# Three experts of a float32 mixture on 64 slots, chosen on the chip, and weight pieces of 1024 columns

## The chip, the core and the metric

The kernel runs on one core of a Trainium2 chip. A time is in microseconds (us) of the device for one execution. The core's engines are TensorE (PE; its weight loads are shown as PEld), VectorE (DVE), ScalarE (ACT), GpSimd (POOL) and SyncE (SP), whose queue issues the weight transfers.

## The reference, cut to what matters

Two decoder layers over 256 tokens of 1024 features; the second layer's channel mixer is a mixture of eight experts, of which each token takes two. In float32:

```
logits = x @ router_w                          # [256, 8]
top_val, top_idx = top_k(logits, 2)
gates = softmax(top_val)
for each token t and each of its two experts e:
    out[t] += gate * (silu(x[t] @ w_gate[e]) * (x[t] @ w_up[e])) @ w_down[e]
x = layer_norm(ALPHA * x + out, ln2_g, ln2_b)
```

`w_gate` and `w_up` are [8, 1024, 3584], `w_down` is [8, 3584, 1024]: 352 MB of float32 for eight experts, each byte read once.

## The kernel before, in words

All weights are split on the chip into a high part, rounded to float32r by ACT (line 173), and the low rest, by DVE (line 176). Tokens are split likewise. A product is the sum of three: high by high, high weights by low tokens, low weights by high tokens (`xstat`, with `mm` at line 97).

Weights come in pieces of 1 MiB (`load`, line 158, on SP's queue) into slots `raw` of rings: 7 slots of `ring`, 7 of `ring2`, and one taken once. `halves` splits a piece into two pairs `wh`, `wl` of 128 x 1024, each with four buffers (`WB`).

Ahead of the experts, `enter_moe` makes the layer norm and the logits, `route` the expert ranks: `place` [token, expert] is 1 plus the token's rank in the expert, or 0. `experts` then goes over experts 0 to 7 in turn. Two experts at a time get their tokens by a product with one-hot slots `D` (`dispatch`), 128 slots each, into `xg`. Of the 3584 inner features a chunk is 512: four pieces of four 128-row blocks by 512 columns for gate (`ps_mm`) and up (`ps_gd`), then silu on ACT (line 1017), the product with up on DVE (1018), four transposes on PE (1024), the split of the transposed `hT` on ACT and DVE (1026, 1027). The down products (`ps_b`, two pieces of two 128-row blocks by 1024 columns) run one chunk late, between these steps. After an expert's last chunk `combine` brings its output back to the tokens by the transposed slots `DT` and adds it, times the gate, to `x_tok` (line 990). The order on each engine follows the program, except where the scheduler moves an instruction that is not pinned.

If some expert has more than 128 tokens, a second pass over the next 128 slots runs behind a branch (lines 1125, 1126).

Of the kernel before, what the change touches and what calls it, by code (L numbers as in the profile page):

```python
# [8 lines left out]
F32 = mybir.dt.float32  # L9
F32R = mybir.dt.float32r  # L10
# [6 lines left out]
P = 128  # L17
# [14 lines left out]
# the constant table: identity, 32 rotary frequencies, further [P, P] matrices, then [P, 32] tiles  # L32
# [31 lines left out]
def trunk(ctx, tc, x, positions, w_in, conv_w, a_log, dt_bias, gdn_norm_w, lam_q1, lam_k1, lam_q2, lam_k2,  # L64
# [35 lines left out]
    def wstat(banks, wh, wl, xT, k0, nk, cols, outs):  # L100
        """Feature-major products, weights stationary: outs = (bank, offset, opens the bank) per 128 columns."""
# [27 lines left out]
    def xlast(outs, xT, subs, b, K, k0=0, n0=0):  # L129
        """The last products of block b, one column part after the other; subs: (k, high, low), all of 128 rows."""  # L130
# [8 lines left out]
    extra = []  # ring2, while it is open  # L139
    turn = [0]  # L140
    once = []  # slots to be taken once, after all the others
    fence_high = [None]  # an ACT instruction that further high parts are issued behind
    fence = [None]  # a DVE instruction that further low parts are issued behind

    def load(src, nk, cols, parts=1, cut=1):
        """One piece of weights, [P, nk, cols] in DRAM, comes in; cut: its second half in so many parts of columns."""
        if once and turn[0] == RING + RING2:
            pool = once.pop()
        else:
            pool = extra[0] if extra and SLOTS[turn[0] % len(SLOTS)] == "x" else ring  # L150
            turn[0] += 1
# [11 lines left out]
    def halves(ld, cut=1, count=2):  # L163
        """The halves of a piece, or a small one as a whole: (first k, high part, low part)."""
# [20 lines left out]
    pre_ctx = ExitStack()  # what the layers ahead of the experts need  # L185
# [37 lines left out]
    def xt_block(xT, src, b, on_pe=True, tags=("mm", "gd")):  # L223
        """One block of 128 tokens of src [P, D] goes to feature-major xT."""
# [25 lines left out]
    def layer_norm(xt, halves, par, dst=None):  # L250
        """LN(ALPHA * xt + halves) into dst (or xt[P, D]), halves: two [P, 512] parts; without halves LN(xt)."""
# [18 lines left out]
    def mixer(l, xT, mx, zab=None):  # L270
# [10 lines left out]
        # --- z gate and the a, b columns, token-major: silu(z) * norm weight  # L281
# [19 lines left out]
        # --- gates: beta, log decay, its running sum  # L301
# [13 lines left out]
        V.scalar_tensor_tensor(e1, lg, -1.0, e1, op0=ALU.add, op1=ALU.subtract)  # rounding of 1 + e, negated  # L315
# [8 lines left out]
        gs = gt[:, 4]  # running sum  # L324
# [6 lines left out]
        # --- decays within a chunk of 128, transposed: [j, i] = exp(G_i - G_j), j <= i  # L331
# [24 lines left out]
        # --- from here on in steps, issued in the order that ORDER says  # L356
        # the activation tables: batches of silus, and of exponentials and logarithms, in turn
# [12 lines left out]
        # --- gated-DeltaNet projections, feature-major, then conv + silu  # L370
# [46 lines left out]
        def with_k(y, o):  # L417
            """(y k^T . decay)^T but for the norm of y."""
# [19 lines left out]
        def with_queries():  # L438
# [3 lines left out]
            G.tensor_tensor(egb, gq[:, :, P:], egb, op=ALU.mult)  # q exp(G) of block 1  # L442
# [57 lines left out]
            # blocks of 64  # L500
# [25 lines left out]
            # blocks of 128  # L526
# [13 lines left out]
        # --- attention projections, token-major  # L540
# [44 lines left out]
        # --- differential attention: scores and softmax  # L585
# [3 lines left out]
        def lambdas():  # L589
# [9 lines left out]
            V.tensor_scalar(lam[:, 5:6], lam[:, 4:5], lam_init, None, op0=ALU.subtract)  # -lambda  # L599
# [322 lines left out]
    def experts(xs, gate, place, mp, ring2, rest, first):  # L922
# [72 lines left out]
        for e in range(NE):  # L995
            j = e % 2
            if j == 0:
                xgs = nxt
# [252 lines left out]
```

## Time and profile before

| | us |
|---|---|
| median of 3 runs | 1547.65 |
| lowest and highest | 1545.3, 1548.48 |
| the profiled execution's span, first to last instruction | 1546.8 |

The profiled execution is known by its span, which lies between the lowest and the highest run; the median is 0.9 us above it. In the rows below, a time is counted from the span's start, "x24" is a count of instructions, and "<-" behind an idle time names what ended it. PE's products are pipelined, so that the duration of a single one (394 ns) is longer than the distance from one to the next.

### The profile page before, as it was taken

The page shows a single profiled execution, that of the slowest core. Times are in us where ns is not written, and L with a number is a line of the kernel's source. Part 1 is how long each engine was busy: PE and PEld are TensorE (multiplying, and loading weights), DVE is VectorE, ACT ScalarE, POOL GpSimd, SP SyncE. Part 2 cuts the span into 40 slices and gives each one's busy share as a digit, 9 for nine tenths or more (in the row PEclk, how much of TensorE's full clock was granted, in tenths as well). Part 3 has the DMA queues.
Part 4 walks back from the last instruction along what each step waited for, and adds up shares of the span by engine and source line. Part 5 has one row for each costly group of instructions (what it writes and reads, how often), then busy time and mean ns, then how long its engine had stood idle before and what let it go on. Part 6 is the DMA issues. An engine that isn't in the chain of part 4 may idle for free.

```text
span 1546.8 us, 23384 instructions
## 1 busy us (share of the span) xinstructions
PE 1507.5 (97%) x8952; PEld 1263.1 (82%) x8952; DVE 1249.1 (81%) x1528; ACT 1054.3 (68%) x1456; POOL 23.6 (2%) x36
## 2 busy tenths in 40 slices
PE   7999999999999999999999999999999999999997
PEld 7978899998978888878878878887887887887885
DVE  4797655556796888897898889889989889888987
ACT  3648544456757587777777777777777777777774
POOL 1000000000100000000000000000000000000000
PEclk9999999999999899999999999999999999999998
DMA  9534465546433799999999999999999999999960
GB/s 306 202 98 130 161 200 187 182 126 215 164 111 137 272 340 350 370 335 338 368 334 356 370 345 360 331 373 345 349 370 349 326 362 333 363 373 332 376 248 30
DMA packets 184695, 433.81 MB, mean 280 GB/s; under 512 B 7400, under 2 KB 9576, under 8 KB 184576
## 3 DMA queue, kind: packets, MB, share of 16 engines
q1 hardware_dynamic: 183392, 428.54, 77.5%
q0 software_dynamic: 1184, 3.71, 0.9%
q8 instruction: 72, 1.18, 0.3%
q14 instruction: 47, 0.39, 0.1%
HBM read 431.17 MB, written 1.05 MB: 279 GB/s over the span
## 4 chain that ended last, share of the span: by engine, by line
PE 93%; DVE 3%; ACT 2%; issue 1%; DMA 1%; SPq 0%; DVEq 0%; ACTq 0%
PE ps_b L97 27%; PE ps_mm L97 27%; PE ps_gd L97 27%; PE ps_a L97 9%; PE ps_a L1024 2%; DVE wl L176 1%; DMA x_in<-in_x_dram 1%; ACT wh L173 1%; DVE x_in L990 0%; PE ps_mm L562 0%; ACT junk L411 0%; PE ps_gd L404 0%; PE ps_mm L666 0%; DVE o L1084 0%; ACT junk L651 0%
## 5 line engine op out<-in xcount | busy, mean ns | idle before, releaser
L176 DVE TENSOR_TENSOR wl<-raw,wh 128x1024 fp32r<-128x1024 f32 (+1 forms) x811 | 948.2, 1219 | 131.9 <-ACT wh L173 124.2
L173 ACT ACTIVATE wh<-raw 128x1024 fp32r<-128x1024 f32 (+1 forms) x811 | 830.4, 1058 | 223.4 <-PE ps_gd L97 109.2
L97 PE MATMUL ps_b<-wh,hT 128*128 128x512 f32 x984 | 273.7, 399 | 0.0
L97 PE MATMUL ps_mm<-wh,xg 128*128 128x512 f32 x896 | 248.4, 394 | 0.0
L97 PE MATMUL ps_gd<-wh,xg 128*128 128x512 f32 x896 | 245.2, 394 | 0.0
L97 PEld LDWEIGHTS ps_b<-wh,hT 128*128 128x128 f32 x984 | 180.7, 188 | 38.0
L97 PEld LDWEIGHTS ps_gd<-wh,xg 128*128 128x128 f32 x896 | 168.2, 188 | 39.0
L97 PEld LDWEIGHTS ps_mm<-wh,xg 128*128 128x128 f32 x896 | 167.4, 188 | 37.9
L97 PE MATMUL ps_b<-wl,hT 128*128 128x512 f32 x492 | 155.0, 394 | 0.0
L97 PE MATMUL ps_gd<-wl,xg 128*128 128x512 f32 x448 | 140.6, 395 | 7.1 <-DVE wl L176 7.1
L97 PE MATMUL ps_mm<-wl,xg 128*128 128x512 f32 x448 | 141.3, 394 | 0.2
L1026 ACT ACTIVATE hT<-ps_a 128x512 fp32r<-128x512 f32 x56 | 33.5, 598 | 130.7 <-PE ps_a L1024 130.6
L97 PEld LDWEIGHTS ps_b<-wl,hT 128*128 128x128 f32 x492 | 92.4, 188 | 21.7
L97 PEld LDWEIGHTS ps_gd<-wl,xg 128*128 128x128 f32 x448 | 83.7, 188 | 29.6 <-DVE wl L176 10.2
L97 PEld LDWEIGHTS ps_mm<-wl,xg 128*128 128x128 f32 x448 | 83.7, 188 | 20.7 <-DVE wl L176 1.5
L1018 DVE TENSOR_TENSOR hh<-hh,ps_gd 128x512 f32<-128x512 f32 x56 | 38.5, 687 | 40.4 <-PE ps_gd L97 40.0
L97 PE MATMUL ps_mm<-xT,wh 128*128 128x256 f32 x448 | 71.0, 280 | 0.0
L1027 DVE TENSOR_TENSOR hT<-ps_a,hT 128x512 fp32r<-128x512 f32 x56 | 38.7, 690 | 38.2 <-ACT hT L1026 38.2
L97 PEld LDWEIGHTS ps_mm<-xT,wh 128*128 128x128 f32 x448 | 60.8, 189 | 0.4
L97 PE MATMUL ps_gd<-xT,wh 128*128 128x256 f32 x320 | 50.5, 280 | 0.0
L97 PE MATMUL ps_mm<-xT,wl 128*128 128x256 f32 x224 | 44.7, 280 | 0.0
L97 PEld LDWEIGHTS ps_gd<-xT,wh 128*128 128x128 f32 x320 | 43.1, 189 | 0.0
(370 smaller groups left out, 1519.3 us busy)
## 6 DMA issues: line engine op xcount, KB each, us to landing
raw<-in_moe_w_gate_dram SPq DMA_DIRECT2D x110, 1024.0 KB, 7.5
raw<-in_moe_w_up_dram SPq DMA_DIRECT2D x110, 1024.0 KB, 6.3
raw<-in_moe_w_down_dram SPq DMA_DIRECT2D x108, 1024.0 KB, 7.3
raw<-in_w_in_dram SPq DMA_DIRECT2D x24, 1024.0 KB, 6.0
raw<-in_ffn_w_gate_dram SPq DMA_DIRECT2D x11, 1024.0 KB, 5.1
raw<-in_ffn_w_up_dram SPq DMA_DIRECT2D x11, 1024.0 KB, 5.2
raw<-in_ffn_w_down_dram SPq DMA_DIRECT2D x11, 1024.0 KB, 5.0
raw<-in_w_out_dram SPq DMA_DIRECT2D x8, 1024.0 KB, 5.0
```

The source lines that it names most:

```text
L97: return PE.matmul(o, lhsT, rhs, start=start, stop=stop, skip_group_check=True)
L173: high = S.activation(wh[:, c:c + n], w, AF.Copy)
L176: low = V.tensor_tensor(wl[:, c:c + n], w, wh[:, c:c + n].bitcast(F32), op=ALU.subtract)
L1018: pin(V.tensor_tensor(hh, hh, pgu[1], op=ALU.mult))
L1024: PE.transpose(pt[:, f * P:(f + 1) * P], hh[:, f * P:(f + 1) * P], ident)
L1026: S.activation(hT[:, :, 0], pv, AF.Copy)
L1027: V.tensor_tensor(hT[:, :, 1], pv, hT[:, :, 0].bitcast(F32), op=ALU.subtract)
```

## The change

Narrow experts: the three experts of 1 to 7 that fewest tokens chose are treated with 64 slots, and their stationary tile holds the 64 high and the 64 low token parts side by side, 128 columns. One product with the high and one with the low weights then gives the high tokens' sum in the output's rows 0 to 63 and the low tokens' in rows 64 to 127. For gate and up, ACT copies the lower rows to SBUF and PE adds them to the upper ones by a shift matrix (`lead`); for down, the transposed slots stand twice in `DT`, so that the combination adds both. Low weights by low tokens come into the sum too.

The experts 1 to 7 are sorted by count on DVE (`order_by_count`); SP loads the number of the expert of a rank into a register, by which its weights are addressed. Expert 0 stays first and wide; then come the ranks in the order of `TURN`: 1, 4, 2, 5, 3, 6, 7, the ranks 1 to 3 narrow. `dispatch` is called for groups: expert 0, then [1, 2], [3, 4], [5, 6] and [7] of the turns.

Gate and up pieces are two 128-row blocks by 1024 columns; an expert has three chunks of 1024 columns and one of 512, with four down pieces (two for the last) in each. The rings have 7 and 6 slots, and the slot taken once goes. Behind the experts there are two passes over all of them, each in a branch of its own: for tokens beyond the 64 or 128 slots, and for those 128 further on.

```diff
-RING2 = 7
-SLOTS = "rrrrrxxxrrxxxx"
-RING3 = 1
+RING2 = 6
+SLOTS = "rrrrrxxxrrxxx"
+CHUNKS = (1024, 1024, 1024, 512)
+NARROW = 3
+TURN = (1, 4, 2, 5, 3, 6, 7)
...
+    def gate_pieces():
+
+        n = 2048 // CHUNKS[0]
+        wg = moe_w_gate[0, 0].rearrange("(k p) c -> p k c", p=P)
+        return [piece(wg[:, k:k + n, 0:CHUNKS[0]], n, CHUNKS[0]) for k in (0, n)]
...
+        count = mp.tile([P, NE], F32, name="count")
+        pin(V.tensor_copy(count, pr[:, 16:24]))
...
+        def order_by_count(gate):
+            places, gates, index, beyond = order_by_count.tiles
+            N = NE - 1
+            w = mp.tile([P, 5, N], F32, name="sortw")
+            cn, rk, cs, ix = (w[:, i] for i in range(4))
+            sq = mp.tile([P, 2, N, N], F32, name="sorts")
+            pm = sq[:, 1]
+            def rows(a, n=N):
+                return a.unsqueeze(2).broadcast_to([P, n, n])
+            def cols(a, n=N):
+                return a.unsqueeze(1).broadcast_to([P, n, n])
+            V.tensor_copy(cn, count[:, 1:NE])
+            V.tensor_tensor(sq[:, 0], cols(cn), rows(cn), op=ALU.is_equal)
+            V.tensor_tensor(sq[:, 0], sq[:, 0], tie[:, 0:N, 0:N], op=ALU.mult)
+            V.tensor_tensor(sq[:, 1], cols(cn), rows(cn), op=ALU.is_lt)
+            V.tensor_tensor(sq[:, 0], sq[:, 0], sq[:, 1], op=ALU.add)
+            V.tensor_reduce(rk, sq[:, 0], axis=AX.X, op=ALU.add)
+            V.tensor_scalar(beyond[:, 1:NE], rk, float(NARROW), -64.0, op0=ALU.is_lt, op1=ALU.mult)
+            V.tensor_scalar(beyond[:, 1:NE], beyond[:, 1:NE], float(P), None, op0=ALU.add)
+            V.memset(beyond[:, 0:1], float(P))
+            V.tensor_scalar(rk, rk, 1.0, None, op0=ALU.add)
+            V.tensor_tensor(pm, cols(rk), rows(io1[:, 0:N]), op=ALU.is_equal)
+            V.tensor_tensor(sq[:, 0], pm, cols(io1[:, 0:N]), op=ALU.mult)
+            V.tensor_reduce(ix, sq[:, 0], axis=AX.X, op=ALU.add)
+            V.tensor_copy(index, ix[0:1])
+            for b in range(NB):
+                for to, of in ((places, place), (gates, gate)):
+                    V.tensor_tensor(sq[:, 0], pm, cols(of[:, b, 1:NE]), op=ALU.mult)
+                    V.tensor_reduce(to[:, b, 1:NE], sq[:, 0], axis=AX.X, op=ALU.add)
+            V.tensor_tensor(cn, cn, beyond[:, 1:NE], op=ALU.subtract)
+            V.tensor_reduce(cs[:, 0:1], cn, axis=AX.X, op=ALU.max)
+            V.tensor_scalar(cs[:, 1:2], count[:, 0:1], float(-P), 0.0, op0=ALU.add, op1=ALU.max)
+            V.tensor_tensor(cs[:, 0:1], cs[:, 0:1], cs[:, 1:2], op=ALU.max)
+            most = mp.tile([1, 1], I32, name="most")
+            V.tensor_copy(most, cs[0:1, 0:1])
...
+        C2 = [(sum(CHUNKS[:i]), n) for i, n in enumerate(CHUNKS)]
...
+        def slots(Dt, job, twice=False):
+            _, where, _, narrow = job
+            w = 64 if narrow else P
+            m = 2 if narrow and twice else 1
+            return V.tensor_tensor(Dt.rearrange("p b (m s) -> p b m s", s=w),
+                                   io1[:, 0:w].unsqueeze(1).unsqueeze(1).broadcast_to([P, NB, m, w]),
+                                   where.unsqueeze(3).broadcast_to([P, NB, m, w]), op=ALU.is_equal)
...
+        def in_pieces(w, c0, cols, parts=1, k0=0):
+            nk = 2048 // cols
+            for k in range(k0, KD, nk):
+                for j, wh, wl in piece(w[:, k:k + nk, c0:c0 + cols], nk, cols, parts):
+                    yield k + j, nk // 2, wh, wl
+        def products(outs, xg, narrow, k, nk, wh, wl, cols):
+            if not narrow:
+                xstat(outs, [xg[:, 0:4], xg[:, 4:8]], k, nk, 0, wh, wl, cols, KD)
+                return
+            for j in range(nk):
+                x_ = xg[:, k + j].rearrange("p c s -> p (c s)")
+                for w in (wh, wl):
+                    for i, o in enumerate(outs):
+                        mm(o, x_, w[:, j * cols + i * 512:j * cols + (i + 1) * 512], k + j == 0 and w is wh, False)
...
+        def down(subs, n, c, hT, py):
+            f0 = C2[c][0] // P
+            for f, wh, wl in subs:
+                if jobs[n][3]:
+                    x_ = hT[:, f].rearrange("p c s -> p (c s)")
+                    for w in (wh, wl):
+                        for i, o in enumerate(py):
+                            mm(o, x_, w[:, i * 512:(i + 1) * 512], f0 + f == 0 and w is wh,
+                               f0 + f == FE // P - 1 and w is wl)
...
+        def lead(p, room, i):
+            hi = slice(64, P)
+            o = room[hi, i * 512:(i + 1) * 512]
+            pin(S.activation(o, p[hi, :], AF.Copy))
+            return lambda: mm(p[0:64, :], shift[hi, 0:64], o, False, True)
+        groups = [[0], [1, 2], [3, 4], [5, 6], [7]] if NARROW and rest else [[n] for n in range(NE)]
...
+        for n, job in enumerate(jobs):
+            narrow = job[3]
+            rows = slice(0, 64) if narrow else slice(0, P)
+            xg = xgs.pop(n)
+            wg, wu = (weights(n, i).rearrange("(k p) c -> p k c", p=P) for i in range(2))
+            for c, (c0, cols) in enumerate(C2):
+                nb = cols // 512
+                pg = [bank("mm") for _ in range(nb)]
+                pu = [bank("gd") for _ in range(nb)]
+                parts = 2 if (n, c) == (NE - 1, len(C2) - 1) else 1
+                hh = mp.tile([P, max(CHUNKS)], F32, tag="hh", name=nm("hh"))
+                if narrow:
+                    hT = mp.tile([P, 2, cols], F32R, tag=f"hT{q % 2}", name=nm("hT"))
+                    room = hT[:, 1]
+                    hT = hT[:, 0].rearrange("p (f c s) -> p f c s", c=2, s=64)
+                nk = 2048 // cols
+                begun = [(i * nk + k0, nk // 2, wh, wl) for i, f in enumerate(first or ()) for k0, wh, wl in f]
+                for sub in begun:
+                    products(pg, xg, narrow, *sub, cols)
+                for sub in in_pieces(wg, c0, cols, parts, len(first or ()) * nk):
+                    products(pg, xg, narrow, *sub, cols)
+                first = None
+                moves = []
+                for s, sub in enumerate(in_pieces(wu, c0, cols, parts)):
+                    products(pu, xg, narrow, *sub, cols)
+                    left = KD // (nk // 2) - s
+                    if narrow and left == 3:
+                        moves = [lead(p, room, i) for i, p in enumerate(pg)]
+                    if narrow and left == 2:
+                        for move in moves:
+                            move()
+                downs = down_pieces(pend[0], pend[1], 1) if pend else iter(())
+                subs = next(downs, None)
+                if narrow:
+                    for i, p in enumerate(pg):
+                        pin(S.activation(hh[rows, i * 512:(i + 1) * 512], p[rows, :], AF.Silu))
+                    moves = [lead(p, room, i) for i, p in enumerate(pu)]
+                else:
+                    for i, p in enumerate(pg):
+                        pin(S.activation(hh[:, i * 512:(i + 1) * 512], p, AF.Silu))
+                if subs:
+                    down(subs, *pend)
+                for move in moves if narrow else ():
+                    move()
+                for i, p in enumerate(pu):
+                    h = hh[rows, i * 512:(i + 1) * 512]
+                    pin(V.tensor_tensor(h, h, p[rows, :], op=ALU.mult))
+                if narrow:
+                    subs = next(downs, None)
+                    if subs:
+                        down(subs, *pend)
+                else:
+                    hT = mp.tile([P, cols // P, 2, P], F32R, tag=f"hT{q % 2}", name=nm("hT"))
+                w = 64 if narrow else P
+                nf = 512 // w
+                for f0 in range(0, cols // P, nf):
+                    n_ = min(nf, cols // P - f0)
+                    pt = bank("a")
+                    for f in range(n_):
+                        PE.transpose(pt[:, f * w:(f + 1) * w], hh[rows, (f0 + f) * P:(f0 + f + 1) * P], ident[rows, rows])
+                    pv = pt[:, 0:n_ * w].rearrange("p (f s) -> p f s", s=w)
+                    S.activation(hT[:, f0:f0 + n_, 0], pv, AF.Copy)
+                    V.tensor_tensor(hT[:, f0:f0 + n_, 1], pv, hT[:, f0:f0 + n_, 0].bitcast(F32), op=ALU.subtract)
+                    subs = next(downs, None)
+                    if subs:
+                        down(subs, *pend)
+                for subs in downs:
+                    down(subs, *pend)
+                if pend and pend[1] == len(C2) - 1:
+                    combine(pend[0], q - 1, pend[3], DT)
+                if c == 1:
+                    DT = transposed(n)
+                if c == 2 and n + 1 < NE and n + 1 not in xgs:
+                    group = groups.pop(0)
+                    xgs = dict(zip(group, dispatch([jobs[g] for g in group])))
+                pend = (n, c, hT, py)
+                q += 1
...
+            def expert_of(r):
+                return lambda: nc.values_load(index[0:1, r - 1:r], engines=(mybir.EngineType.SP,), min_val=1, max_val=NE - 1)
+            jobs = every[:1] + [job(expert_of(r), r, places, gates, r <= NARROW) for r in TURN]
+            most = experts(xs, jobs, mp, ring2, then, first)
...
+        for turn_ in range(2 if NARROW else 1):
+            with tc.If(n > turn_ * P):
+                if turn_ or not NARROW:
+                    V.tensor_scalar(place, place, float(-P), None, op0=ALU.add)
+                else:
+                    V.tensor_tensor(place, place, beyond.unsqueeze(1).broadcast_to([P, NB, NE]), op=ALU.subtract)
+                experts(xs, every, mp, ring2, None, None)
```

## Rows read from the trace of the kernel before

**Rows 1.** The page, span and busy time, share, instructions of each engine
```profile
span 1546.8 us, 23384 instructions
...
PE 1507.5 (97%) x8952; PEld 1263.1 (82%) x8952; DVE 1249.1 (81%) x1528; ACT 1054.3 (68%) x1456; POOL 23.6 (2%) x36
```

**Rows 2.** Windows: stretch, its length, busy time by engine, PEclk, DMA share, GB/s
```profile
560.00:1450.00 890.00, 882.69 (x3954) 715.66 (x3953) 786.92 (x751) 671.25 (x761) 0.00 (x0) 1.00 0.97 351
...
603.00:671.00 68.00, 68.00 (x303) 55.25 (x302) 59.75 (x59) 51.06 (x57) 0.00 (x0) 1.00 1.00 367
```

**Rows 3.** The page, the chain that ended last, by engine
```profile
PE 93%; DVE 3%; ACT 2%; issue 1%; DMA 1%; SPq 0%; DVEq 0%; ACTq 0%
```

**Rows 4.** The chain in order of time, 514 to 580: start, us, what
```profile
559.46 0.44 PE ps_a L1024 x4
...
568.25 5.56 PE ps_gd L97 x24
```

**Rows 5.** Timeline of DVE at the first three combinations: start, us, line, what
```profile
668.96 1.41 DVE L990 SCALAR_TENSOR_TENSOR x_in<-ps_a,route,x_in 128x512 f32<-128x512 f32 x2
...
796.08 1.41 DVE L990 SCALAR_TENSOR_TENSOR x_in<-ps_a,route,x_in 128x512 f32<-128x512 f32 x2
...
919.83 1.41 DVE L990 SCALAR_TENSOR_TENSOR x_in<-ps_a,route,x_in 128x512 f32<-128x512 f32 x2
```

**Rows 6.** Groups by form, ACT and DVE, 520 to 1540: busy, mean ns, idle before
```profile
L1026 ACT ACTIVATE hT<-ps_a 128x512 fp32r<-128x512 f32 x56 | 33.5, 598 | 130.7 <-PE ps_a L1024 130.6
L1017 ACT ACTIVATE hh<-ps_mm 128x512 f32<-128x512 f32 x56 | 32.4, 579 | 0.0
...
L176 DVE TENSOR_TENSOR wl<-raw,wh 128x1024 fp32r<-128x1024 f32 x671 | 778.1, 1219 | 28.6 <-ACT wh L173 24.9 <-PE ps_a L97 2.5
L1027 DVE TENSOR_TENSOR hT<-ps_a,hT 128x512 fp32r<-128x512 f32 x56 | 38.7, 690 | 38.2 <-ACT hT L1026 38.2
L1018 DVE TENSOR_TENSOR hh<-hh,ps_gd 128x512 f32<-128x512 f32 x56 | 38.5, 687 | 40.4 <-PE ps_gd L97 40.0
L990 DVE SCALAR_TENSOR_TENSOR x_in<-ps_a,route,x_in 128x512 f32<-128x512 f32 x28 | 19.7, 747 | 4.9 <-PE ps_a L97 4.0
L984 DVE TENSOR_TENSOR ys<-ps_b,ys 128x512 fp32r<-128x512 f32 x14 | 9.6, 683 | 0.0
```

**Rows 7.** Timeline of DVE and ACT, splits issued back to back
```profile
674.02 6.89 DVE L176 TENSOR_TENSOR wl<-raw,wh 128x1024 fp32r<-128x1024 f32 x6
...
1504.98 5.79 ACT L173 ACTIVATE wh<-raw 128x1024 fp32r<-128x1024 f32 x6
```

**Rows 8.** Windows at the filling of the rings, columns as in rows 2
```profile
506.00:512.00 6.00, 6.00 (x28) 4.87 (x27) 4.23 (x7) 0.50 (x2) 0.00 (x0) 1.00 1.04 414
512.00:522.00 10.00, 9.75 (x52) 8.04 (x50) 8.14 (x13) 3.27 (x7) 0.00 (x0) 0.83 1.04 388
```

**Rows 9.** Timeline of SP's queue at the filling of the rings
```profile
503.95 1.35 SPq L158 DMA_DIRECT2D raw<-in_moe_w_down_dram  x2
505.40 1.03 SPq L158 DMA_DIRECT2D raw<-in_moe_w_gate_dram  x2
506.48 6.59 SPq L158 DMA_DIRECT2D raw<-in_moe_w_up_dram  x2
```

**Rows 10.** Timeline of DVE in the routing
```profile
524.85 0.35 DVE L886 TENSOR_TENSOR compare<-compare,tie 128x64 f32<-128x64 f32 x2
```

**Rows 11.** Instructions of the branch's line: ns min/median/max, first and last start
```profile
L1126 SPq EVENT_SEMAPHORE  x8: 17/17/17, 1544.5 to 1545.1; - x8
...
L1126 PEldq COMPARE_BRANCH  x1: 3407/3407/3407, 1531.4 to 1531.4; - x1
...
L1126 SPq COMPARE_BRANCH  x1: 50/50/50, 1541.5 to 1541.5; - x1
```

**Rows 12.** Windows in the second mixer, columns as in rows 2
```profile
450.00:460.00 10.00, 9.43 (x290) 7.21 (x289) 9.29 (x19) 2.26 (x3) 0.00 (x0) 1.00 0.34 109
470.00:480.00 10.00, 10.00 (x56) 8.23 (x56) 6.33 (x19) 7.22 (x22) 0.00 (x0) 0.83 0.22 82
```

More of the change, by code (lines that the diff above doesn't have):

```diff
@@ L145, in load @@
     def load(src, nk, cols, parts=1, cut=1):
[L147 to L151, printed above, removed]
+        pool = extra[0] if extra and SLOTS[turn[0] % len(SLOTS)] == "x" else ring
+        turn[0] += 1
         raw = pool.tile([P, WC], F32, tag="raw", name=nm("raw"))
@@ L853, in enter_moe @@
         logits(0)
-        first = [gate_piece(0, 0, half) for half in range(2)]
+        first = gate_pieces()
         busy(8)
@@ new lines, in route, with experts, xg_tile, dispatch @@
+        if NARROW:
+            sorted_ = mp.tile([P, 2, NB, NE], F32, name="sorted")
+            order_by_count.tiles = (sorted_[:, 0], sorted_[:, 1], mp.tile([1, NE - 1], I32, name="index"),
+                                    mp.tile([P, NE], F32, name="beyond"))
+        return gate, place, rest, order_by_count
+    def experts(xs, jobs, mp, ring2, rest, first):
+        C2 = [(sum(CHUNKS[:i]), n) for i, n in enumerate(CHUNKS)]
+        def xg_tile(narrow):
+            xg_turn[0] += not narrow
+            return mp.tile([P, KD, 2, 64 if narrow else P], F32R, tag="xgn" if narrow else f"xg{xg_turn[0] % 2}", name=nm("xg"),
+                           bufs=1)
+        def slots(Dt, job, twice=False):
[5 more added lines that the diff above has]
+                                   where.unsqueeze(3).broadcast_to([P, NB, m, w]), op=ALU.is_equal)
+        def dispatch(group, early=False):
+            ws = [64 if job[3] else P for job in group]
+            W = sum(ws)
+            Dt = mp.tile([P, NB, W], F32R, tag="hh", name=nm("D"))
+            for j, job in enumerate(group):
+                fence[0] = pin(slots(Dt[:, :, sum(ws[:j]):sum(ws[:j + 1])], job))
+            xgs = [xg_tile(job[3]) for job in group]
@@ L971, in down_piece @@
-        def down_piece(e, c, half, parts=1, cut=1):
-            wd = moe_w_down[0, e].rearrange("(f p) d -> p f d", p=P)
-            return list(piece(wd[:, 4 * c + 2 * half:4 * c + 2 * half + 2, :], 2, D, parts, cut))
-        def down(subs, half, e, c, hT, py):
-            for j, wh, wl in subs:
-                xstat(py, [hT], 2 * half + j, 1, 0, wh, wl, D, FE // P, 4 * c)
-        def combine(e, py, DT):
-            for n in range(2):
-                ys = mp.tile([P, 2, 512], F32R, tag=f"hT{e % 2}", name=nm("ys"))
+            for b in range(NB):
+                PE.transpose(pt[:, b * P:(b + 1) * P], Dt[:, b].bitcast(F32), ident)
@@ new lines, in down_pieces @@
+        def down_pieces(e, c, parts=1, cut=1):
+            wd = weights(e, 2).rearrange("(f p) d -> p f d", p=P)
+            c0, cols = C2[c]
+            for f in range(0, cols // P, 2):
+                last = f == cols // P - 2
+                yield [(f + j, wh, wl) for j, wh, wl in piece(wd[:, c0 // P + f:c0 // P + f + 2, :], 2, D, parts,
+                                                              cut if last else 1)]
+        def down(subs, n, c, hT, py):
[8 more added lines that the diff above has]
+                else:
+                    for w in (wh, wl):
+                        for c_ in range(2 if w is wh else 1):
+                            for i, o in enumerate(py):
+                                mm(o, hT[:, f, c_], w[:, i * 512:(i + 1) * 512], f0 + f == 0 and w is wh and c_ == 0,
+                                   f0 + f == FE // P - 1 and w is wl)
@@ L1042, in experts @@
+                pend = (n, c, hT, py)
+                q += 1
+        _, where, gate, _ = job
+        f0 = C2[c][0] // P
+        subs = [(f0 + f, wh, wl) for subs in down_pieces(n, c, 2, 2) for f, wh, wl in subs]
         extra.clear()
@@ L1100, in experts, with moe @@
         return most
[L1102 to L1113 removed]
+    xg_turn = [0]
+    def moe(xs, pl, first, mp, ring2):
+        gate, place, rest, order_by_count = route(pl, mp)
         def then():
             most = rest()
+            if NARROW:
+                most = order_by_count(gate)
             for b in range(NB):
@@ L1183, in trunk @@
     io1 = cpool.tile([P, P], F32, name="io1")
+    shift = cpool.tile([P, 64], F32R, name="shift") if NARROW else None
     def router_constants():
```

156 lines of the change are left out of this document (49 added, 107 removed).

## Prediction

> **What bounds the kernel now.** I read the page's head first: of a span of 1546.8 us TensorE (PE) is busy for 97%, VectorE (DVE) for 81%, ScalarE (ACT) for less [rows 1]. A PE that is busy on average need not be the bound in the stage that is changed, so I then cut out the eight experts. In the 890 us from 560 to 1450 PE is busy 882.7 us, DVE 786.9, ACT 671.3, the granted clock is 1.00 (2.4 GHz), and the DMA share is 0.97 at 351 GB/s; in an undisturbed stretch of 68 us PE has no gap at all while the transfers run at share 1.00 and 367 GB/s [rows 2]. The reader should see three resources close together: PE full, DMA nearly full, DVE at 88%. The chain that ended last says which one counts: 93% of it is PE [rows 3]. Its pieces give PE's price: 24 products of 512 columns take 5.56 us, 0.232 us each, and the four transposes of a chunk 0.44 us [rows 4]. A chunk of 512 columns has 72 products (24 gate, 24 up, 24 down): 72 x 0.232 + 0.44 = 17.1 us. The pace of whole experts stands in the timeline of DVE, where each expert's first addition to the tokens starts at 668.96, 796.08, 919.83 us [rows 5]: 127.1 us for an expert with a dispatch of the next pair in it, 123.7 without, 250.9 a pair. So what is to be saved is PE work, until DVE or DMA takes over.
>
> **The change part by part: PE.** A narrow expert has its high and low token parts side by side in one stationary tile of 64 + 64 columns, so that a weight row needs two products (with its high and its low part) where it needed three. Per 512 columns that is 48 products instead of 72, plus two products by the shift matrix that add the lower half of gate and up to the upper: 50 x 0.232 + 0.44 = 12.0 us, or 7 x 12.0 + 8 x 0.232 for the combination = 86 us an expert [rows 4]. Three of eight experts fall by some 38 us of PE work. That is not the gain, because the weights are the same bytes and must still be split.
>
> **DVE, the next bound.** Each expert has 84 halves of 1024 columns to split into a low part. One is 1219 ns long [rows 6], but issued back to back six take 6.89 us, 1.148 each [rows 7]. 84 x 1.148 = 96.4. Then 7 products of silu and up at 0.687 (half the partitions, as many columns): 4.8. The low parts of the transposed product are half as wide: three of 512 columns at 0.690 and one of 256, taken as 0.4: 2.5. The combination, 4 x 0.747 + 2 x 0.683: 4.4 [rows 6]. Slots and their transposed copy, two operations of 256 columns: 0.8. Sum 109 us. This is the least that a narrow expert can take. ACT by the same count: 84 high parts at 0.965 (six in 5.79 us [rows 7]), 7 silus at 0.579, 14 new copies out of PSUM ahead of the shift, priced as the silu, 4 + 2 operations at 0.598 [rows 6]: 97 us, below DVE.
>
> **What is late on DVE.** To the 109 us come its waits. The idle columns show 40.4 us before the product with up, 38.2 before the low part of hT and 28.6 before splits over the 56 chunks [rows 6], 1.9 us a chunk. The new wait lies here: ACT's copy of up's lower half waits for PE's last up product, PE's shift for ACT, DVE's product for the shift. Behind ACT's copy stand the high parts of the next down pieces, behind PE's shift the next down products, behind DVE's product the next splits. Laid end to end the path is four products of the last half (0.93), the two copies (1.16), two shifts (0.46), two products (1.37), eight narrow transposes (at most 2 x 0.44 = 0.9 [rows 4]), hT on ACT and DVE (0.6 + 0.69): 6.1 us, against eight down halves, 8 x 1.148 = 9.2 us of splitting, that can be put between its links. A narrow expert now has four chunks (three of 1024 columns, one of 512). From below the waits are nothing (109 us); from above the whole path stands bare in each, 4 x 6.1 = 24 us (133 us). I take 1.25 us a chunk, less than now, because DVE is now the late engine and only its turn-round with PE is left: 5 us, N = 114.
>
> **Wide experts.** Their products, transposes and splits are as many as before, in chunks twice as wide. Nothing is saved. The dispatch goes from pairs of 256 columns to groups of 192, all in wide experts: 3.4 us becomes some 2.6; the last expert's own dispatch gives this back. DVE's clusters (two products, 1.37 us) are covered by the four buffers of split weights, which PE takes 1.39 us each to use (six products). So a pair of wide and narrow takes 123.7 + 2.6 + N and saves 124.5 - N = 10.5 us; three pairs save 31.5.
>
> **Transfers.** A narrow expert's 42 pieces of 1 MiB (44.0 MB) in 114 us ask for 386 GB/s; a pair asks for 88.1 MB in 240 us, 367 GB/s, which the 68 us stretch already holds [rows 2]. The excess inside a narrow expert, 19 GB/s x 114 us = 2.2 MB, is two of the thirteen slots, and the order of turns gives each narrow expert a wide one ahead of it in which to fill them. More is available: when the ring is filled at the start, the window in which down rows (4 KB each) were first in the queue moved 414 GB/s and the next, of gate and up rows (2 KB), 388 [rows 8, 9]. Gate and up in 1024 columns have rows of 4 KB as well. Hence nothing for DMA, its bound being 44.0 / 0.388 = 113.5 us and, by the faster row, 106 us, before any help from the ring. The Trainium skill, "DMA: Bandwidth & Descriptors", section Specifications, puts HBM at about 358 GB/s for a core, against this change: by it a pair could not be under 88.1 / 0.358 = 246 us and a pair would save 4.8, and the time would be 1547.7 - 14.3 + 3.5 = 1537. The trace does not agree over short stretches (414, 388 and 367 GB/s); none of its rows shows such a rate held for hundreds of us.
>
> **Choosing the experts.** The order of counts adds 27 small DVE operations and takes two away, 0.1 to 0.2 us each by operations of 64 columns, where two take 0.35 [rows 10]: 2.5 to 5 us, at the start of expert 0, where DVE already keeps PE's first products waiting. Between nothing (fitted into gaps) and 5 I take 2. The first dispatch, of one expert and not two, halves its copies and columns: 0 to 2.6 us, taken as 1.5 back. SP's load of an expert's number stands ahead of all later weight loads on SP's queue, but the number is ready in the first 20 us of expert 0, and SP comes to it when the 42nd piece is due, some 80 us later: nothing; without that cover, the landing of one transfer, once.
>
> **The end.** There are now two branches around passes that are not run. At the one of before PE's branch took 3.4 us, and SP, last, went on 3.0 us after its own [rows 11]. A second in series costs 0 (if both are fetched together) to 3.4 us, I take 3. The passes are not run: the reference's router, on the inputs as they are drawn, gives 79, 75, 77, 58, 32, 80, 29, 82 tokens, so the three smallest of experts 1 to 7 (29, 32, 58) fit 64 slots and the rest 128.
>
> **Sum.** 1546.8 - 31.5 + 2 - 1.5 + 3 = 1518.8 us in the profiled execution's terms. The median shown, 1547.65, is 0.9 above that span; I carry it over: 1520 us. With N at 109 and the small costs at nothing, 1546.8 - 46.5 - 1.5 + 0.9 = 1500; with N at 118 and the small costs at their upper ends 1546.8 - 19.5 + 8.4 + 0.9 = 1537. That is the forecast's own range.
>
> **Rivals.** (1) Transfers take over. For it: share 0.97 at 351 GB/s over 890 us [rows 2], which scaled to a full share is 362. A pair then takes 88.1 / 0.362 = 243.4 us, saves 7.5, and the time is 1547.7 - 22.5 + 3.5 = 1529. Against it: the share passed 1.00 at 388 and 414 [rows 8]. The figure of the Trainium skill above ("DMA: Bandwidth & Descriptors", Specifications) is this rival's harder form, and its 1537 lies in the range. (2) DVE's waits eat it all: at 3.3 us of idle a chunk N is 122.2, three pairs save 7, the small costs take half and the time is within 3 us of before, 1544. For it: 1.9 a chunk now, and two more links in the path; against it the 9.2 us of splitting to put between. (3) Slower: the path stands bare. From N = 124.4 on (3.9 us a chunk) the kernel is slower by over 3 us; with all 6.1 us N is 133, and the time 1547.7 + 25.5 + 3.5 = 1577. What decides is whether DVE's in-order queue has splits between the product and the low part of hT. (4) The clock. PE would wait some 0.2 us behind each half in a narrow expert. It was granted 1.00 in a stretch of 290 small products with gaps (9.43 of 10 us), and 0.83 in a later one of 56 [rows 12]. At 1.2 GHz a narrow expert's PE work would be 2 x 86 = 172 us, and the time 1547.7 + 3 x 47.5 + 3.5 = 1694.
>
> **How the numbers follow.** Two medians of this kernel are told apart from about 0.2%, 3 us. Chances: forecast 0.58, rival 1 0.19, rival 2 0.08, rival 3 0.12, rival 4 0.03. The first two are faster by over 0.2%, the third is within it, the last two slower: 0.77, 0.08, 0.15. The range from 1500 to 1548 takes in the forecast's range, rival 1 and rival 2, and leaves out rivals 3 and 4 and a little below.
>
> **What would show it.** Right: in the profile after, DVE's first additions to the tokens stand about 126 and 114 us apart in turn; in narrow stretches DVE is busiest (over 0.93), PE has gaps that end with splits, and the DMA rate is above 370 GB/s. The page has some 430 matmuls fewer than 8952 [rows 1]: 3 x 7 x 22, less the 32 of a fifth dispatch. Wrong: narrow stretches of 120 us and more with DVE idle before its product with up or before hT (waits), or with SP free and high parts waiting for landings (transfers), or with a granted clock under 1.00.

## The result, and the profile after

The median fell from 1548.07 us (1545.3 to 1552.62) to 1530.09 us (1529.51 to 1530.5), four runs of each: a ratio of 0.9885, with a 95% interval of 0.9862 to 0.9907. The profiled execution's span is 1528.3 us, 18.5 below that of before; forecast were 28.0. The kernel before is timed anew in every round, on several chips, and its median lies between 1546.6 and 1548.1 us. One execution of e1 below took 1691.2 us at a granted clock of 0.80 and is left out of e1's numbers.

The page's head and its chain by engine:

```profile
span 1528.3 us, 23267 instructions
...
PE 1459.9 (96%) x8522; PEld 1164.7 (76%) x8522; DVE 1248.0 (82%) x1553; ACT 1079.5 (71%) x1494; POOL 23.7 (2%) x36
...
PE 82%; DVE 9%; ACT 4%; issue 2%; DMA 2%; SPq 0%; DVEq 0%; ACTq 0%
```

8952 - 8522 = 430 matmuls fewer, as counted beforehand. Against [rows 1, 3] PE's share of the chain is down from 93 to 82%, and DVE's is up from 3 to 9%: another engine has begun to end waits.

DVE's first additions to the tokens, the pace of whole experts (timeline of DVE):

```profile
684.55 1.40 DVE L1082 SCALAR_TENSOR_TENSOR x_in<-ps_a,route,x_in 128x512 f32<-128x512 f32 x2
798.70 1.40 DVE L1082 SCALAR_TENSOR_TENSOR x_in<-ps_a,sorted,x_in 128x512 f32<-128x512 f32 x2
924.32 1.40 DVE L1082 SCALAR_TENSOR_TENSOR x_in<-ps_a,sorted,x_in 128x512 f32<-128x512 f32 x2
1038.67 1.40 DVE L1082 SCALAR_TENSOR_TENSOR x_in<-ps_a,sorted,x_in 128x512 f32<-128x512 f32 x2
```

The steps are 114.2, 125.6 and 114.4 us where "126 and 114" was written, and a pair is 239.8 where [rows 5] gave 250.9. Such a step runs from the middle of one first chunk to the next, so it mixes two experts. Cut at each expert's first gate product instead, a narrow expert takes 110.1 us and a wide one 128.0 to 131.7. The windows of two narrow experts and of the wide one between them (columns as in [rows 2]):

```profile
657.70:767.90 110.20, 103.80 (x398) 66.03 (x397) 104.69 (x102) 97.23 (x112) 0.00 (x0) 0.98 1.00 384
897.50:1007.60 110.10, 104.42 (x397) 67.11 (x396) 104.61 (x102) 97.40 (x111) 0.00 (x0) 0.97 1.00 385
1007.60:1139.40 131.80, 128.22 (x568) 102.45 (x567) 114.75 (x111) 98.89 (x118) 0.00 (x0) 0.99 0.93 349
```

In the narrow expert DVE is busy 104.6 of 110.1 us (95%), ACT 97.4, and the DMA share is 1.00 at 385 GB/s. DVE and the transfers are nearly full; windows alone can't say which of them sets the 110.1. PE's 104.4 is not work of that size: its column counts each product up to its end, which at full pace is later than the start of the next one, and so short waits do not show in it. They show at the weight loads (PEld) of the same expert, in the timeline and in the waits (us in total, times, longest):

```profile
940.19 0.30 PEld L99 LDWEIGHTS ps_gd<-wl,xg 128*128 128x128 f32 x2 [0.38 <-DVE wl L174]
940.19 0.73 PE L99 MATMUL ps_gd<-wl,xg 128*128 128x512 f32 x2
940.75 0.63 PE L99 MATMUL ps_gd<-wh,xg 128*128 128x512 f32 x2
...
942.94 0.63 PE L99 MATMUL ps_gd<-wl,xg 128*128 128x512 f32 x2
943.41 0.40 PE L99 MATMUL ps_gd<-wh,xg 128*128 128x512 f32 x1
```

```profile
PEld ps_mm L99 <- DVE wl L174: 8.6, 17, 1.7
PEld ps_b L99 <- DVE wl L174: 7.4, 18, 0.8
PEld ps_gd L99 <- DVE wl L174: 7.2, 18, 0.8
```

From 940.19 to the next start two products take 0.56 us, and 0.47 from 942.94, where none waits. In the whole expert the weight loads wait 23.2 us for DVE's low parts. That is the mechanism of the prediction: PE's gaps end with splits.

Where the loss lies, a stretch of PE, ACT and DVE at expert 0's third chunk, in which the next pair's tokens are dispatched (start, us, idle before in brackets), a window over its end, and one over the same row in the next wide expert:

```profile
627.05 1.03 PE L99 MATMUL ps_a<-D,xs 128*128 128x192 f32 x8
...
629.66 0.69 PE L99 MATMUL ps_a<-D,xs 128*128 128x192 f32 x4 [0.70 <-ACT xg L1016]
...
631.05 1.14 PE L99 MATMUL ps_a<-D,xs 128*128 128x192 f32 x8 [0.70 <-ACT xg L1016]
...
633.96 1.96 PE L99 MATMUL ps_mm<-wh,xg 128*128 128x512 f32 x4
...
635.96 1.06 ACT L171 ACTIVATE wh<-raw 128x1024 fp32r<-128x1024 f32 x1 [1.21 <-PE ps_mm L99]
...
637.05 1.23 DVE L174 TENSOR_TENSOR wl<-raw,wh 128x1024 fp32r<-128x1024 f32 x1 [5.24 <-ACT wh L171]
```

```profile
631.00:636.00 5.00, 4.75 (x21) 4.20 (x22) 0.82 (x1) 2.58 (x11) 0.00 (x0) 0.67 1.00 376
...
870.00:875.00 5.00, 3.41 (x25) 2.90 (x24) 2.45 (x2) 4.33 (x15) 0.00 (x0) 1.00 1.01 360
```

The dispatch's 32 products stand in one row on PE and take from 627.05 to 633.96, 6.9 us, because PE waits for ACT to copy each bank into `xg`. Meanwhile no split weights are used up, so ACT's next high part waits for PE and DVE idles 5.24 us; and the granted clock averages 0.67 over the 5 us from 631, so that part of them ran at 1.2 GHz. Behind the gaps four products take 1.96 us instead of 1.09. The clock is the smaller part: the same row in the next wide expert (868.5 to 874.8 us, with the same waits) keeps 1.00 and takes 6.3 us. In the trace of before a dispatch of a pair took turns with gate products (from 720 to 727 us two of them, eight of the dispatch, two, eight, and so on) and cost the 3.4 us between its two kinds of expert [rows 5]:

```profile
720.78 1.11 PE L97 MATMUL ps_a<-D,xs 128*128 128x256 f32 x8
721.73 0.64 PE L97 MATMUL ps_mm<-wh,xg 128*128 128x512 f32 x2
722.21 1.25 PE L97 MATMUL ps_a<-D,xs 128*128 128x256 f32 x8
```

The end, by the second branch's line (ns min/median/max, first and last start):

```profile
L1280 PEldq COMPARE_BRANCH  x2: 3502/4032/4561, 1509.6 to 1513.8; - x2
...
L1280 SPq COMPARE_BRANCH  x2: 45/49/53, 1519.6 to 1523.3; - x2
```

Two branches stand in series. PE's two, 3.5 and 4.6 us, are over by 1518.4, before DVE's last operation ends (1519.20); SP's second comes 3.7 us after its first, behind that end. From DVE's end to the span's end are 9.1 us; before they were 5.6.

### The profile page after: what moved, and what is told of

Its sections match the earlier page's. It is cut to its first block, busy times and chain, and to the rows that moved or that the text cites. A ratio compares the mean times of both kernels' runs of the same rounds, so it can differ in the third digit from the quotient of the medians.

```text
span 1528.3 us, 23267 instructions
## 1 busy us (share of the span) xinstructions
PE 1459.9 (96%) x8522; PEld 1164.7 (76%) x8522; DVE 1248.0 (82%) x1553; ACT 1079.5 (71%) x1494; POOL 23.7 (2%) x36
## 4 chain that ended last, share of the span: by engine, by line
PE 82%; DVE 9%; ACT 4%; issue 2%; DMA 2%; SPq 0%; DVEq 0%; ACTq 0%
PE ps_gd L99 25%; PE ps_mm L99 25%; PE ps_b L99 21%; PE ps_a L99 9%; DVE wl L174 5%; ACT wh L171 2%; DMA raw<-in_moe_w_up_dram 1%; PE ps_a L1168 1%; DMA x_in<-in_x_dram 1%; DVE hT L1171 1%; DVE hh L1155 1%; DVE x_in L1082 1%; ACT xg L1016 0%; PE ps_mm L560 0%; DVE ys L1076 0%
## 5 line engine op out<-in xcount | busy, mean ns | idle before, releaser
L99 PE MATMUL ps_b<-wh,hT 128*128 128x512 f32 x816 | 235.1, 400 | 0.3
L99 PE MATMUL ps_mm<-wh,xg 128*128 128x512 f32 x728 | 216.3, 404 | 2.4 <-ACT wh L171 2.4
L99 PE MATMUL ps_gd<-wh,xg 128*128 128x512 f32 x728 | 207.3, 394 | 0.0
L99 PEld LDWEIGHTS ps_b<-wh,hT 128*128 128x128 f32 x816 | 151.6, 189 | 38.1 <-ACT wh L171 3.1
L99 PE MATMUL ps_b<-wl,hT 128*128 128x512 f32 x492 | 164.3, 414 | 10.0 <-DVE wl L174 9.7
L99 PEld LDWEIGHTS ps_mm<-wh,xg 128*128 128x128 f32 x728 | 138.8, 193 | 35.1 <-ACT wh L171 4.1
L99 PEld LDWEIGHTS ps_gd<-wh,xg 128*128 128x128 f32 x728 | 136.7, 188 | 31.7
L1170 ACT ACTIVATE hT<-ps_a 128x512 fp32r<-128x512 f32 (+1 forms) x47 | 27.3, 583 | 53.5 <-PE ps_a L1168 53.3
L1155 DVE TENSOR_TENSOR hh<-hh,ps_gd 128x512 f32<-128x512 f32 (+1 forms) x56 | 36.2, 681 | 26.3 <-PE ps_gd L99 21.8
L1171 DVE TENSOR_TENSOR hT<-ps_a,hT 128x512 fp32r<-128x512 f32 (+1 forms) x47 | 31.2, 667 | 14.3 <-ACT hT L1170 14.3
```

The source lines that it names most:

```text
L99: return PE.matmul(o, lhsT, rhs, start=start, stop=stop, skip_group_check=True)
L1155: pin(V.tensor_tensor(h, h, p[rows, :], op=ALU.mult))
L1170: S.activation(hT[:, f0:f0 + n_, 0], pv, AF.Copy)
L1171: V.tensor_tensor(hT[:, f0:f0 + n_, 1], pv, hT[:, f0:f0 + n_, 0].bitcast(F32), op=ALU.subtract)
```

## The experiments

All are timed against the kernel before on the same chip. Expert lengths are from first gate product to first gate product, "wide" being those between narrow ones (in e2 and e11 all experts after expert 0).

| run | median us | ratio to before, 95% | expert 0 | narrow | wide |
|---|---|---|---|---|---|
| before | 1548.07 | 1 | 115.3 | none | 127.0 / 123.8 |
| the change | 1530.09 | 0.9885 [0.9862, 0.9907] | 124.7 | 110.1 | 128.0 to 131.7 |
| e1 narrow, pieces of 512 | 1533.41 | 0.9907 [0.9879, 0.9936] | 122.1 | 112.3 to 115.0 | 126.4 to 128.3 |
| e2 pieces of 1024 alone | 1577.99 | 1.0198 [1.0167, 1.0229] | 123.6 | none | 128.6 |
| e3 one branch | 1527.35 | 0.9877 [0.984, 0.9913] | 124.7 | 110.1 | 128.0 to 131.6 |
| e4 dispatch in steps | 1517.94 | 0.9811 [0.9782, 0.984] | 120.1 | 110.1 | 126.8 to 127.2 |
| e5 fewer low parts | 1511.53 | 0.9774 [0.9753, 0.9795] | 124.7 | 104.1 | 127.9 to 131.6 |
| e6 order known | 1530.42 | 0.9893 [0.9877, 0.991] | 124.7 | 110.1 | 128.1 to 131.3 |
| e7 steps and one branch | 1515.34 | 0.9796 [0.978, 0.9812] | 120.0 | 110.1 | 126.8 to 127.3 |
| e8 as e7, pieces of 512 | 1521.36 | 0.9834 [0.9818, 0.9851] | 120.6 | 113.1 to 116.0 | 125.2 to 125.6 |
| e9 a sixth on POOL | 1589.95 | 1.0294 [1.0265, 1.0323] | 120.2 | 131.8 to 135.7 | 127.2 to 128.4 |
| e10 a twelfth on POOL | 1571.49 | 1.0177 [1.015, 1.0203] | 120.3 | 128.9 to 130.3 | 126.8 to 127.2 |
| e11 as e2, dispatch in steps | 1565.76 | 1.0115 [1.0099, 1.0132] | 120.3 | none | 127.4 |

**e1 and e2, the change's two halves.** `CHUNKS = (512,) * 7`, and `NARROW = 0`.

> The narrow experts are kept, all chunks are 512 columns wide as before, so gate and up rows are 2 KB. Theory A (the time missing from the forecast is lost in the dispatches, which stand in one row on PE and wait for ACT's copies; the wide pieces help the narrow experts): a narrow expert has seven turn-rounds of DVE with PE in place of four, at 1.4 us each 4 us more, and its transfers at the 388 GB/s of 2 KB rows take 113.5 us in place of 108; narrow experts 114 to 116 us, time 1541 to 1547. Theory B (the wide chunks themselves slow the wide experts): wide experts come back to some 125 us, narrow stay at 110 to 112, time 1515 to 1525.

> Pieces and chunks of 1024 columns with all eight experts wide, in their own order, one dispatch for each of the experts 1 to 7, no sorting, one branch. Theory A: wide experts are PE-bound as before, 123.7 us, plus seven dispatches in a row at 3 to 5 us each where three cost 3.4 before: 1553 to 1570, slower than before by 5 to 22 us. Theory B: each wide expert 4 us more besides: over 1575.

Narrow experts without the pieces gain 13.4 us (the whole change: 18.0); the pieces alone lose 31 us. Neither theory's time was met in e1, which lies between the two, and e2's 1578 is theory B's number, of which e11 below shows another cause. In e1 a narrow expert moves 368 GB/s against 385 with pieces of 1024; DVE is busy for 107.1 us in it, and whether the transfers or DVE's extra turns hold it at 115 is not shown:

```profile
894.70:1009.70 115.00, 106.95 (x397) 64.00 (x396) 107.13 (x107) 97.43 (x114) 0.00 (x0) 1.00 0.99 368
```

e2 has a dispatch in each of its experts 0 to 6, seven instead of three; e11 below takes that apart.

**e3, the end.** The second pass nested in the first's branch:

```diff
-        for turn_ in range(2 if NARROW else 1):
-            with tc.If(n > turn_ * P):
+        def more(turn_):
+            with tc.If(n > turn_ * P):
...
+                if not turn_:
+                    more(1)
```

> The second extra pass stands inside the first one's branch, so that one branch is passed at the end. If a branch costs each engine its own fetch of code, 2.9 us by SP: 1526.5 to 1527.5, and 2.8 to 3.3 us less between the last DVE operation and the end. If the fetches lie beside the output's transfers: 1530.

```profile
L1280 PEldq COMPARE_BRANCH  x1: 3579/3579/3579, 1507.7 to 1507.7; - x1
...
L1280 SPq COMPARE_BRANCH  x1: 53/53/53, 1517.8 to 1517.8; - x1
```

One branch is left on each queue, and from DVE's last end (1517.35) to the span's end (1522.9) are 5.6 us: 3.5 less than with two in series. The medians differ by 2.7 us, but e3's four times spread from 1524.3 to 1531.9, so that the trace, and e7 below, carry this.

**e4, the dispatch.** `dispatch` becomes a generator that is advanced one block of 128 features after each half's products of the next chunk, with tiles of its own for `D` and one `DT`:

```diff
                 for sub in in_pieces(wg, c0, cols, parts, len(first or ()) * nk):
                     products(pg, xg, narrow, *sub, cols)
+                    next(steps, None)
```

> The eight steps of a dispatch are issued one by one behind the gate and up products of the next chunk, in a tile of their own. Theory A: the four dispatches fall from some 7, 7, 8 and 4 us to 2 to 3 us each, 14 us in all, the clock no longer falls there, wide experts take 123 to 127 us: 1514 to 1519. Theory B (the wide chunks cost the wide experts, whatever the dispatch does): 1526 or more.

The same dispatch as above, PE's timeline (two kinds of product in turn), and the window over all of it:

```profile
626.91 0.25 PE L99 MATMUL ps_a<-D,xs 128*128 128x192 f32 x1
627.00 0.65 PE L99 MATMUL ps_mm<-wl,xg 128*128 128x512 f32 x2
627.48 0.48 PE L99 MATMUL ps_a<-D,xs 128*128 128x192 f32 x3
627.79 1.11 PE L99 MATMUL ps_mm<-wh,xg 128*128 128x512 f32 x4
```

```profile
625.90:640.00 14.10, 14.10 (x77) 12.01 (x76) 12.04 (x11) 11.38 (x24) 0.00 (x0) 1.00 1.03 398
```

PE has no gap, the clock stays at 1.00, and DVE goes on splitting. Expert 0 loses 4.7 us, the wide ones 2.8, 4.4 and 1.1; together 13.0, of which the median shows 12.2. The theory that the row of products costs the gain holds. The tile of its own for `D` is not tested apart, but in the row PE's waits were for ACT's copies alone. The dispatch still costs its products: a last chunk of 512 columns ahead of a narrow expert takes 26.2 us with the steps in it, where it took 22.7 to 23.7.

**e5, what bounds a narrow expert.** One low part in six is not computed in the narrow experts (the product with it uses the high part again):

```diff
+            if left_out:
+                high = S.activation(wh[:, :m], raw[:, i * m:i * m + m], AF.Copy)
+                yield i * (nk // count), wh, wh[:, :]
+                continue
```

> The changed kernel, but in the narrow experts one half in six has no low part: the subtraction on DVE is left out and the products read the high part a second time, so that TensorE's work, the transfers and ACT's work stay as they are. Some 14 subtractions of 1.2 us, about 17 us of DVE's 104.6 us in a narrow expert, go. What bounds a narrow expert at 110.1 us? Theory A, DVE's subtractions with short waits: a narrow expert falls to TensorE's own sum, about 104.5 to 106 us, and the whole kernel by 12 to 15 us, to about 1516 us. Theory B, the transfers (44 MB at the 406 to 409 GB/s that the full stretches show is about 108 us): the expert stays at 108 to 110 us, the kernel at 1524 to 1530 us, and the waits on DVE's subtractions turn into waits on transfers.

```profile
656.70:760.80 104.10, 98.58 (x397) 67.55 (x396) 90.59 (x89) 96.22 (x111) 0.00 (x0) 0.98 1.02 393
891.90:996.00 104.10, 98.61 (x397) 67.34 (x396) 90.60 (x89) 96.25 (x111) 0.00 (x0) 0.98 1.01 392
```

The same bytes, products and high parts now take 104.1 us: 6 less in each, 18.6 in the median, a little more than theory A's 12 to 15. So the low parts on DVE held the narrow experts, and the transfers, which here ran at 392 GB/s, did not. The edit also takes one buffer of `wl` less in six; but in the changed kernel DVE waits for other things than a free buffer (waits of DVE from 897.5 to 1007.6: us, times, longest):

```profile
DVE hh L1155 <- PE ps_gd L99: 4.8, 4, 1.9
DVE wl L174 <- ACT wh L171: 0.8, 3, 0.5
```

That it stops at 104.1, with ACT at 96.2 busy, shows no single next bound; the DMA share, 1.02, is the fullest.

**e6, choosing on the chip.** Ranks replaced by a list, the ranking and SP's loads of a number left out:

```diff
-            jobs = every[:1] + [job(expert_of(r), r, places, gates, r <= NARROW) for r in TURN]
+            by_count = (6, 4, 3, 1, 2, 5, 7)
+            jobs = every[:1] + [job(by_count[r - 1], by_count[r - 1], place, gate, r <= NARROW) for r in TURN]
```

> The changed kernel with the order of the experts written in (6, 4, 3 first, then 1, 2, 5, 7, the order by count of these inputs), in the same turn and with the same pair, so that ranking, sorting and the loads of an expert's number are left out; the reduction that gates the second pass counts against 128 as before. Theory A, choosing on the chip costs what its small operations on DVE take ahead of the first chunk, about 2 us, and nothing later: the kernel gains 1 to 3 us, to about 1528 us, all of it in job 0. Theory B, the number's load holds up the queue that issues the transfers, at each expert's start: 5 to 10 us less, found at the starts of experts. Theory C: no difference that can be measured.

Theory C: 1530.42 against 1530.09, and expert 0 as long as with the sorting (124.7).

**e7 and e8, both edits, and the size of the pieces again.** e7 is e3 and e4 together; e8 is e7 with `CHUNKS = (512,) * 7`.

> The two edits that gained by themselves, together: the dispatch one step at a time between the next chunk's products, and the second pass's branch inside the first's. If the gains add (12 us and 3 us off 1530.1), 1514 to 1516 us. Rival: the two overlap at the end, or the queues' order changes with the branch, and it stays at 1518 us.

> The same two edits with gate and up weights in pieces of 512 columns throughout. Theory A, the pieces of 1024 columns earn only in the narrow experts, whose transfers they quicken (115 against 110 us), and cost little in the wide ones once the dispatch is spread: 3 x 4.5 us more in the narrow experts, 5 x 1 us less in the wide ones, about 1523 us. Rival: the wide experts win as much as the narrow ones lose (2 to 3 us each), and it equals the run with pieces of 1024, 1515 us.

The gains add: 1515.3 is the best time of a version that leaves nothing out. In e7's trace 5.5 us lie behind DVE's end where e4 has 9.2. Pieces of 1024 columns shorten a narrow expert by 3 to 6 us and lengthen a wide one by 1.5; in all they are worth 6.0 us.

**e9 and e10, DVE's work given to POOL.** On e7, every sixth or twelfth low part of the narrow experts:

```diff
+                if pool_turn:
+                    tc.keep_in_program_order(
+                        G.tensor_tensor(wl[:, c:c + n], w, wh[:, c:c + n].bitcast(F32), op=ALU.subtract))
+                    continue
```

> The version with both edits (1515.3 us), and in the narrow experts every sixth subtraction on POOL, which the trace shows idle there; nothing is left out. POOL's operations on 128x512 numbers took 1.1 to 1.3 us at the start of the kernel, so one half should take some 2.4 us, and there are 7 us from one to the next. If DVE's own time is what holds a narrow expert at 110.1 us, it falls to TensorE's 104 us as where the low parts were left out: 18 us less, about 1497 us. Rival: POOL's subtractions slow DVE's beside them, or come late for TensorE: if one takes 5 us or more, or DVE's operations stretch by a sixth, the gain is gone, and the experts stay at 108 to 112 us, 1512 to 1522 us.

> The same with every twelfth subtraction on POOL. DVE is relieved of some 8.5 us in a narrow expert, more than the 6 us that separate it from TensorE's 104 us: if both engines stay as quick as apart, 104 to 106 us and 1498 to 1503 us; with the rival of the run before, half of its loss.

The rival, and far beyond its price: a narrow expert takes 132 to 136 us and 129 to 130. With half the subtractions on POOL, e10 still loses 56.2 of e9's 74.6 us. Two stretches of e9 (timelines of DVE, PE and POOL):

```profile
780.25 6.88 DVE L183 TENSOR_TENSOR wl<-raw,wh 128x1024 fp32r<-128x1024 f32 x6
...
782.58 6.76 POOL L181 TENSOR_TENSOR wl<-raw,wh 128x1024 fp32r<-128x1024 f32 x1 [6.73 <-ACT wh L176]
...
789.39 1.22 PE L99 MATMUL ps_b<-wl,hT 128*128 128x512 f32 x2 [4.41 <-POOL wl L181]
```

```profile
684.65 2.41 POOL L181 TENSOR_TENSOR wl<-raw,wh 128x1024 fp32r<-128x1024 f32 x1 [8.74 <-PE ps_a L99]
...
686.32 1.83 DVE L183 TENSOR_TENSOR wl<-raw,wh 128x1024 fp32r<-128x1024 f32 x1
```

Started ahead of DVE's next subtraction, POOL takes 2.41 us. Begun beside the third of six subtractions of DVE back to back, it ends 2.2 us after the last of them (789.34 against 787.13), so it has waited for the four that were left, which kept their pace (six in 6.88 us); PE, whose order is fixed, then waits 4.41 us. The other way round DVE's subtraction, started while POOL ran, lasts 1.83 us, 0.6 more, and ends 1.1 us after POOL (688.15 against 687.06). Each holds the other off for whole operations, and POOL did not get in between DVE's. In the first narrow expert of e9 (135.7 us) PE waits 16.8 us for POOL's low parts, and its granted clock is 0.91. The Trainium skill, "SBUF — State Buffer", section "SBUF: two separate sides", says that DVE and GpSimd share a port pair as an exclusive lock, taken by a DVE operation with two SBUF inputs against a GpSimd operation that reads SBUF, and that the loser blocks for the whole instruction; both stretches agree.

**e11, the pieces without the row.** e2 with e4's edit.

> No narrow expert, no choosing, pieces of 1024 columns (the run with pieces alone, 1578.0 us, experts of 128.6 us), with each expert's dispatch one step at a time between the next chunk's gate and up products. Theory A, that run lost its 31 us to its dispatches in one row (seven in place of three): an expert falls to 126 to 127 us, which is 123.8 and 32 products of a dispatch, and the kernel to 1561 to 1567 us; what then remains against before (some 15 us) is four dispatches more. Theory B, pieces of 1024 columns themselves slow the wide experts, by coarser interleaving on DVE: the experts stay at 128 us or more, the kernel above 1573 us.

An expert falls from 128.6 to 127.4 us and the kernel by 12.2, to 1565.8. Theory A's range for the kernel holds, its range for an expert is missed by 0.4: the row in e2 cost 1.2 us an expert, while most of what was lost is the dispatches themselves, one an expert in place of one a pair. Of the 3.6 us above 123.8, a dispatch's 32 products explain 3.1, 0.39 us for four (timeline of PE):

```profile
885.31 0.56 PE L99 MATMUL ps_a<-D,xs 128*128 128x128 f32 x4
885.70 1.15 PE L99 MATMUL ps_mm<-wh,xg 128*128 128x512 f32 x4
```

That leaves 0.5 us a wide expert to the pieces themselves here, against 1.5 between e7 and e8. PE's idle time (an expert's window less PE's busy time in it) points the same way: 0.9 us in a wide expert of e11, 1.8 in e7, 0.5 in e8. Why a wide expert pays more behind a narrow one stays open.

## Why the prediction held, and where its sum was off

The mechanism is the one described (PE's products fall, DVE's splits become the bound of a narrow expert), and the range held the time; 9.5 us are missing in the span (1528.3 against 1518.8). By stretches:

- **Three pairs**: forecast to save 31.5, saved 752.6 - 719.8 = 32.8, but by two errors that cancel. N was put at 114 and is 110.1: DVE's work is 104.6, not 109, while its waits are 5.5 us, almost the 5 taken. The wide experts between them were put at 126.3 and are 129.8 on average: the dispatch. That the sign "126 and 114" came out as 125.6 and 114.2 is therefore partly luck.
- **Expert 0**: forecast +2 - 1.5 = +0.5; it is longer by 124.7 - 115.3 = 9.4. This is the step that failed: "3.4 us becomes some 2.6; the last expert's own dispatch gives this back". Two things are wrong in it. A chunk with the dispatch of a pair takes 41.1 to 42.0 us, against 34.5 with none in it (e4), so that a dispatch costs some 7 us and not 2.6; it was priced by its products, while the order on PE, all in one row against ACT's copies, sets its time. And the dispatch inside expert 0, which it did not have before, was set off against a saving that the pairs' term had already counted, so it stood in the sum nowhere. Of the 9.4 us some 2.4 are left over, which are not the sorting (e6); where they lie stays open.
- **The sorting**, taken as 2 us, cost nothing that e6 can measure. SP's load of a number cost nothing, as written. The 1.5 us taken back for the first dispatch are not seen either: the first gate product starts 0.4 us earlier than before (532.98 against 533.34).
- **The last expert and the end**: +5.2 against +3. The second branch is 3.5 of it (e3), well sized; the other 1.7 stay open.

On the rivals: rival 1's number, 1529, was met within 1.1 us, but not its mechanism: a pair takes 239.9 us on average, not 243.4, and e5 leaves the transfers as they are and gains 18.6 us. It holds 392 GB/s for 104 us, twice. So rival 1 fell, and with it the rule cited there from the Trainium skill, "DMA: Bandwidth & Descriptors", section Specifications (about 358 GB/s a core): for this one core at work it is no limit. A time that fits a rival's sum does not show the rival. Rivals 2 and 3 fell with DVE's idle time, 1.4 us a chunk. Rival 4 appeared in small, and with it one of the prediction's signs of being wrong (a granted clock under 1.00): the clock fell, but for a few microseconds at a time; the two narrow experts above kept a mean of 0.98 and 0.97. It did not set their time: in e4 the first of them runs at 1.00 and takes the same 110.1 us:

```profile
652.30:762.40 110.10, 103.33 (x397) 64.48 (x396) 104.61 (x102) 97.35 (x111) 0.00 (x0) 1.00 0.99 384
```

## What to carry to other kernels

Price a moved or regrouped step by where its instructions stand in each engine's order, not by their count: 32 products that wait for another engine's copies cost twice their time (6.9 against 3.4 us) when nothing stands between them, and they starve the engines behind PE. Read PE's load from the distances between its products and the waits of its weight loads, not from its busy time alone: a narrow expert showed 104 us busy although its weight loads waited 23 us for DVE. When several engines are near full, take a sixth of one engine's work away, with all else in place, before naming the bound; here one run showed that the transfers, full in every window, were not it. And count instances: each dispatch, branch and load in the new order, expert by expert.

## What was not expected of the hardware

- POOL is idle for the whole expert stage and yet could take no work from DVE: subtractions of 1.15 us back to back held one of its operations off until the last was through, and with every sixth subtraction on POOL the kernel lost 74.6 us (1589.95 against 1515.34).
- The granted clock fell in two of three rows of 32 small products between which PE had waited 0.2 to 0.7 us at a time: 0.67 over 631 to 636, and 0.70 over 1112 to 1117, but 1.00 over 870 to 875. With the same products spread (e4) it stayed at 1.00.
- With rows of 4 KB the transfers sustained 384 to 393 GB/s over 104 to 110 us.
- Skipped branches are not free: a second one in series added 3.5 us at the end.
